# A first norm whose squares are added in pairs on GpSimd, and an inverse root in nine instructions

## The chip, the core and the metric

The kernel runs on one core of a Trainium2 chip. The metric is device time in microseconds, the median of several runs of the whole program. Before the change it is 1212.53 us (three runs, 1211.41 to 1212.78).

A core has five engines that run side by side: TensorE (PE; its weight loads are listed as PEld), VectorE (DVE), ScalarE (ACT), GpSimd (POOL) and SyncE (SP), which here issues DMAs. Each works through its own queue in order. A tile that is written by one engine and read by another carries a semaphore between them.

## The reference

Two residual layers on a sequence of 512 tokens with 1024 channels. Layer 0 mixes tokens with a grouped state-space layer (S5), layer 1 with forgetting attention; each is followed by a gated feed-forward layer with a short convolution. Every sub-layer is preceded by an RMS norm that is modulated by a conditioning vector `c`, and the trunk ends with one more norm:

```python
def rmsnorm(x, g):
    x32 = x.astype(jnp.float32)
    y = x32 * lax.rsqrt(jnp.mean(x32 * x32, axis=-1, keepdims=True) + EPS)
    return (y * g.astype(jnp.float32)).astype(x.dtype)

def modulate(x, g, shift, scale):
    return rmsnorm(x, g) * (1.0 + scale) + shift

def adaln_params(c, w, b):
    mod = jax.nn.silu(c) @ w + b
    shift, scale, gate = jnp.split(mod, 3, axis=-1)
    return shift[:, None, :], scale[:, None, :], gate[:, None, :]
...
    h = x
    for i in range(DEPTH):
        shift, scale, gate = adaln_params(c, ada_w[i, 0], ada_b[i, 0])
        hn = modulate(h, norm_g[i, 0], shift, scale)
        m = s5_mixer(hn, ...) if i % 2 == 0 else fox_mixer(hn, ...)
        h = h + gate * m
        ...
        h = h + gate * conv_ffn(hn, ...)
    return rmsnorm(h, final_g)
```

There are five norms: two in each layer and the last one. Each needs, for every token, the sum of the squares of 1024 channels and one over the root of its mean.

## The kernel before

The activations lie in SBUF as `h`, eight tiles of 128 channels by 512 tokens, so that the channels of a token are spread over partitions. A sum over channels is therefore a matmul with ones.

**The first norm.** It stands at the start of the S5 layer (`s5`, from L1080), before anything else can run. SyncE loads `h` in four DMAs of two tiles (L134), a pack of small constants (`rest`), and then the adaptive-norm weights, eight tiles of 512 KB for the scale and eight for the shift (`ada_pe`, the DMAs at L186 in `raw`). ScalarE squares one tile of `h` after another (L1113) into the pool tile `nm_t`, which has two buffers, and TensorE adds the tile into `ps` (`mmp`) with a matmul against a tile of ones (L1114). Every fp32 matmul shows as two MATMUL instructions in the trace, called passes below. ScalarE copies the sum to SBUF (L1116), and four transposes (L1119) bring it to one row per token: `stats`.

VectorE meanwhile works out the parameters of the state-space layer in `s5_params` (L824): an exponential, a sine and a cosine on tiles of 128x32, dozens of short instructions with L701 to L756, which are helper lines. It then interleaves two lists of instructions: the inverse root of the norm (`inv_root`, L386, which reads `stats`) and the turn factors (`s5_turns`, L896). After that come more parameters (L853 to L881, `next(params)`), the scale that is applied to the norm (`ga`, L167, in `ada_columns`), and the eight normed tiles `a_x` (L1130).

TensorE's order behind the transposes is: the scale matmuls (L205, with weights in `raw`), the norm broadcast over partitions (`rms_rows`, L410), the columns of the scale (L157, L162), the first shift matmuls, and then the input projection (L1144), which reads `a_x` two tiles at a time with shift matmuls in between. The weights' tiles `raw`, `w_hi` and `w_lo` are rings of three, five and five buffers, so a shift load can wait for a scale matmul.

The block from L1106 is written under `manual_schedule` for TensorE, ScalarE, VectorE and SyncE: their instructions keep the program's order. GpSimd isn't in that list; at the start it has only memsets, and the first time that it works on tiles otherwise is in the attention layer (L1453, an addition, and L1496).

The pool `tp` (`s5t`) holds temporary tiles of this stage; it is closed before the loop over the S5 groups, and `s5r` takes its room. `s5r` tiles wait for the tiles that lay there.

**The other norms.** They are fed from the residual additions: squares are added on VectorE as they arise (`square`), and `rms_stats` sums with a matmul, for each half of the tokens by itself, at the end of the product before it (`product`, `tail`). The first half's root is broadcast in the middle of the second half's matmuls (L331), the second half's is put off until 12 matmul groups of the next product are out (`finish_norm`). The last norm's second half has nothing behind it: its root scales the output (`norm_out`). `inv_root` is called nine times: once in the first norm on 128x4 values and eight times on 128x2.

`inv_root` begins with an integer estimate of one over the root, improves it with a step of third order and then with a Newton step. Its instructions depend on one another.

Of the kernel before, what the change touches and what calls it, by code (L numbers as in the profile page):

```python
# [8 lines left out]
F32 = mybir.dt.float32  # L9
# [3 lines left out]
ALU = mybir.AluOpType  # L13
# [4 lines left out]
P = 128  # L18
D = 1024
KT = D // P  # L20
S = 512
# [52 lines left out]
class Trunk:  # L74
# [311 lines left out]
    def inv_root(self, ps, nb, log=None):  # L386
        v, r, t, y = (self.small.tile([P, nb], I32 if n == "r" else F32, name=f"rs_{n}") for n in "vrty")
        e = self.nc.vector
        f = r.bitcast(F32)
        steps = (  # L390
            lambda: e.tensor_scalar(v, ps, 1.0 / D, EPS, op0=ALU.mult, op1=ALU.add),
            lambda: e.tensor_scalar(r, v.bitcast(I32), -0.5, float(0x5F3759DF), op0=ALU.mult, op1=ALU.add),
            lambda: e.tensor_tensor(t, f, f, ALU.mult),
            lambda: e.tensor_tensor(t, t, v, ALU.mult),
            lambda: e.scalar_tensor_tensor(t, t, -1.25 / 0.375, t, op0=ALU.add, op1=ALU.mult),
            lambda: e.tensor_scalar(t, t, 0.375, 1.875, op0=ALU.mult, op1=ALU.add),
            lambda: e.tensor_tensor(y, f, t, ALU.mult),
            lambda: e.tensor_tensor(t, y, y, ALU.mult),
            lambda: e.tensor_tensor(t, t, v, ALU.mult),
            lambda: e.tensor_scalar(t, t, -0.5, 1.5, op0=ALU.mult, op1=ALU.add),  # L400
            lambda: e.tensor_tensor(y, y, t, ALU.mult),
        )
        in_turn(steps) if log is None else log.extend(steps)
        return y
# [268 lines left out]
def in_turn(*logs):  # L673

    order = sorted(((n + 0.5) / len(l), i, n) for i, l in enumerate(logs) for n in range(len(l)))
    for _, i, n in order:
        logs[i][n]()
# [104 lines left out]
class S5(Trunk):  # L782
# [297 lines left out]
    def s5(self, i, nxt):  # L1080
        nc, tc = self.nc, self.tc
# [4 lines left out]
        with ExitStack() as stack:  # L1086
# [4 lines left out]
            ones = keep.tile([P, P], F32, name="s5_ones")  # L1091
            nc.vector.memset(ones, 1.0)
            self.s5q = spool("s5q", stack)
            with ExitStack() as start:
                tp = spool("s5t", start)
                w = {}

                def load_w(m):
                    w[m] = self.raw([P, KT, P], self.io["s5_w_in"][m], m % 3)

                self.rot = keep.tile([P, 2, G // 2, B], F32, name="s5_rot")
                nc.gpsimd.memset(self.rot[:, 0, :, 0:1], 1.0)
                nc.gpsimd.memset(self.rot[:, 1, :, 0:1], 0.0)
                zero = tp.tile([L - 1, CG * GM], F32, name="s5_zero")
                nc.gpsimd.memset(zero, 0.0)
                with tc.manual_schedule(engines={ENG.PE, ENG.Activation, ENG.DVE, ENG.SP}):  # L1106
                    self.load_x(self.act)
                    self.load_rest()
                    self.s5_planes(keep)
                    ps = self.mm.tile([P, S], F32, name="mmp")  # L1110
                    for k in range(KT):
                        sq = self.tmp.tile([P, S], F32, name="nm_t")
                        nc.scalar.activation(sq, self.h[:, k, :], AF.Square)  # L1113
                        nc.tensor.matmul(ps, ones, sq, start=(k == 0), stop=(k == KT - 1))  # L1114
                    rows = self.tmp.tile([P, S], F32, name="nm_t")
                    nc.scalar.activation(rows, ps, AF.Copy)  # L1116
                    stats = self.aux.tile([P, NB, P], F32, name="aux")
                    for b in range(NB):
                        nc.tensor.transpose(stats[:, b], rows[:, b * P:(b + 1) * P], self.ident)  # L1119
                    params = self.s5_params(keep, tp, self.first["s5_prm"], stats[:, :, 0])  # L1120
                    y = next(params)
                    scale = self.ada_pe(i, (1,), late=True)
                    for _ in range(KT // 2):
                        next(scale)
                    rb = self.rms_rows(y, NB)
                    next(params)
                    next(scale)
                    x = self.act.tile([P, KT, S], F32, name="a_x", tag="a_hi")
                    for k in range(KT):
                        nc.vector.scalar_tensor_tensor(  # L1130
                            x[:, k], self.h[:, k], self.ga[i][:, k:k + 1], rb, op0=ALU.mult, op1=ALU.mult
                        )

                    shift = self.ada_pe(i, (0,), late=True)
                    ps = self.mm.tile([P, S], F32, name="mmp")
                    for k in range(KT):
                        if k % 2 == 0:
                            next(shift)
                        if k == 0:
                            load_w(0)  # L1140
                        if k == 6:
                            self.s5_consts(keep, tp)
                            self.s5_signs_b()
                        nc.tensor.matmul(ps, w[0][:, k, :], x[:, k], start=(k == 0), stop=(k == KT - 1))  # L1144
                    next(shift)
                    load_w(1)
                    nc.sync.dma_start(self.rr[:, 0::2], self.io["s5_c"])
                    nc.sync.dma_start(
                        self.z[:, P:, :].rearrange("m j r -> j m r"), zero[:, None, :].to_broadcast([L - 1, KT, CG * GM])
                    )  # L1150
                    for k in range(2):
                        nc.scalar.activation(x[:, k], x[:, k], AF.Identity, bias=self.par[i][:, k:k + 1])
                    col = self.aux.tile([P, 1], F32, name="aux")
                    for k in range(KT):
                        last_mm = nc.tensor.matmul(
                            col, w[0][:, k, :], self.par[i][:, k:k + 1], start=(k == 0), stop=(k == KT - 1)
                        )
                    shifted = self.small.tile([P, 1], F32, name="u_shift")
                    nc.scalar.activation(shifted, col, AF.Copy)
                    first = self.tmp.tile([P, L, B], F32, name="uf", tag="nm_t")  # L1160
                    nc.scalar.activation(first, ps.rearrange("p (b j) -> p j b", j=L), AF.Identity, bias=shifted)
                    for k in range(2, KT):
                        nc.scalar.activation(x[:, k], x[:, k], AF.Identity, bias=self.par[i][:, k:k + 1])
                    behind = [self.s5_signs_c(), next(params), self.s5_tables(slice(0, G // 2), 0, 3), last_mm.ins]
# [42 lines left out]
            ps = self.aux.tile([KT, P], F32, name="aux")  # L1207
# [63 lines left out]
        with tc.tile_pool(name="s5b", bufs=1, reuse_waits="tile") as pool:  # L1271
# [15 lines left out]
            after, y = nxt  # L1287
# [358 lines left out]
```

## Time and profile before

| | |
|---|---|
| median of three runs | 1212.53 us (1211.41 to 1212.78) |
| profiled execution, its own time | 1215.46 us |
| its span, first to last instruction | 1213.7 us |
| TensorE busy | 1183.8 us (98%), 7793 instructions |
| VectorE busy | 1004.6 us (83%), 1872 instructions |
| ScalarE busy | 610.0 us (50%) |
| GpSimd busy | 85.8 us (7%) |
| first matmul of the first norm | 6.57 us |
| inverse root of the first norm begins | 17.57 us |
| first normed tile begins (L1130) | 26.23 us |

The table's last three rows are starts in the profiled execution, counted from its first instruction. The time of an execution is a little longer than its span, since work lies around it. Busy shares are means over stages with different limits, so the first 45 us have to be read by themselves, engine by engine: which instruction waits, and for whom. In a row of a timeline the first number is the start, the second the length; in brackets stand the idle time just before it on its engine and what ended it.

### The profile page before, as it was taken

The numbers are of one execution on the slowest core, as the hardware profiler recorded it, in microseconds if no ns is written. First come the engines' busy times: TensorE is split into PE (matmuls) and PEld (weight loads), VectorE is DVE, ScalarE is ACT, GpSimd is POOL, SyncE is SP. The second block draws the span as 40 slices with busy tenths as digits, with TensorE's granted clock in tenths as the row PEclk, the third lists the DMA queues.
The fourth block names the chain that finished last, engine by engine and source line by source line (L and its number), as shares of the span: only waits on it lengthen the run. The fifth ranks groups of instructions, "written<-read, shape, count | busy, mean of one in ns | idle before, by whom it ended". The sixth has DMA issues, their size and how long they took to land.

```text
span 1213.7 us, 20336 instructions
## 1 busy us (share of the span) xinstructions
PE 1183.8 (98%) x7793; PEld 1015.9 (84%) x7793; DVE 1004.6 (83%) x1872; ACT 610.0 (50%) x1156; POOL 85.8 (7%) x145
## 2 busy tenths in 40 slices
PE   6999999999999999999999999999999999999997
PEld 2566678898988899789899888878989999999987
DVE  7799987689899988899788578876899887888865
ACT  3554565335545453445443565764466554555543
POOL 0000000100000000000000343520000000000000
PEclk9899999999999999999999999999999999999999
DMA  9588787531364544544435453432213332333331
GB/s 356 188 266 258 245 271 253 202 99 53 122 204 156 179 163 155 161 159 130 131 125 194 162 173 134 150 109 88 89 55 111 117 121 84 104 103 109 109 100 70
DMA packets 74513, 183.81 MB, mean 151 GB/s; under 512 B 23232, under 2 KB 25632, under 8 KB 73392
## 3 DMA queue, kind: packets, MB, share of 16 engines
q1 hardware_dynamic: 68367, 161.02, 40.5%
q0 software_dynamic: 5760, 20.97, 5.4%
q8 instruction: 61, 1.00, 0.3%
q10 hardware_dynamic: 288, 0.52, 0.1%
q14 instruction: 37, 0.30, 0.1%
HBM read 175.57 MB, written 6.92 MB: 150 GB/s over the span
## 4 chain that ended last, share of the span: by engine, by line
PE 62%; issue 26%; DVE 4%; DMA 4%; POOL 2%; ACT 1%; SPq 0%; POOLq 0%; DVEq 0%; ACTq 0%
PE mmp L294 25%; PE mmp L550 11%; PE aux L550 4%; PE mmp L1174 3%; PE mmp L1366 3%; PE mmp L1203 2%; PE aux L1505 1%; PE aux L1525 1%; POOL ada_raw L233 1%; PE aux L1065 1%; PE mmp L205 1%; DMA ada_raw<-in_ada_t 1%; PE aux L978 1%; PE aux L1057 1%; DVE w_lo L278 1%
## 5 line engine op out<-in xcount | busy, mean ns | idle before, releaser
L278 DVE TENSOR_TENSOR w_lo<-raw,w_hi 128x1024 fp32r<-128x1024 f32 (+4 forms) x173 | 183.2, 1064 | 37.6 <-ACT w_hi L277 37.1
L277 ACT ACTIVATE w_hi<-raw 128x1024 fp32r<-128x1024 f32 (+4 forms) x173 | 154.8, 905 | 102.0 <-PE mmp L294 44.5
L294 PE MATMUL mmp<-ghi,w_hi 128*128 128x512 f32 (+1 forms) x392 | 145.1, 370 | 0.0
L294 PE MATMUL mmp<-ghi,w_lo 128*128 128x512 f32 (+1 forms) x392 | 144.3, 368 | 0.7 <-DVE w_lo L278 0.5
L294 PE MATMUL mmp<-glo,w_hi 128*128 128x512 f32 (+1 forms) x392 | 144.6, 369 | 0.0
L294 PE MATMUL mmp<-a_hi,w_hi 128*128 128x512 f32 (+1 forms) x376 | 138.4, 371 | 1.5 <-ACT a_hi L433 1.5
L294 PE MATMUL mmp<-a_hi,w_lo 128*128 128x512 f32 (+1 forms) x376 | 136.1, 362 | 0.3 <-DVE w_lo L278 0.3
L294 PE MATMUL mmp<-a_lo,w_hi 128*128 128x512 f32 (+1 forms) x376 | 135.7, 362 | 0.0
L550 PE MATMUL mmp<-w_hi 128*128 128x256 f32 x396 | 109.9, 278 | 3.0 <-ACT nm_h L557 2.5
L550 PE MATMUL mmp<-w_hi,w_lo 128*128 128x256 f32 x396 | 109.7, 278 | 0.7 <-DVE w_lo L278 0.7
L550 PE MATMUL mmp<-w_lo,w_hi 128*128 128x256 f32 x396 | 109.5, 277 | 0.0
L557 ACT ACTIVATE nm_h<-mmp 128x256 f32<-128x256 f32 x99 | 37.2, 381 | 108.3 <-PE mmp L550 108.3
L278 DVE TENSOR_TENSOR w_lo<-sums,w_hi 128x1024 fp32r<-128x1024 f32 x74 | 90.1, 1220 | 0.0
L277 ACT ACTIVATE w_hi<-sums 128x1024 fp32r<-128x1024 f32 x74 | 77.0, 1054 | 25.3 <-DVE sums L518 23.4
L294 PEld LDWEIGHTS mmp<-ghi,w_lo 128*128 128x128 f32 x392 | 74.2, 189 | 13.9 <-DVE w_lo L278 1.4
L294 PEld LDWEIGHTS mmp<-ghi,w_hi 128*128 128x128 f32 x392 | 74.2, 189 | 11.9 <-ACT w_hi L277 0.6
L294 PEld LDWEIGHTS mmp<-glo,w_hi 128*128 128x128 f32 x392 | 74.2, 189 | 11.0
L294 PEld LDWEIGHTS mmp<-a_hi,w_hi 128*128 128x128 f32 x376 | 70.2, 188 | 13.2 <-ACT a_hi L433 1.9
L294 PEld LDWEIGHTS mmp<-a_hi,w_lo 128*128 128x128 f32 x376 | 70.6, 188 | 12.5 <-DVE w_lo L278 1.3
L294 PEld LDWEIGHTS mmp<-a_lo,w_hi 128*128 128x128 f32 x376 | 70.7, 188 | 9.7
L362 DVE SCALAR_TENSOR_TENSOR h<-mmp,par,h 128x512 f32<-128x512 f32 (+1 forms) x100 | 68.1, 683 | 11.8 <-PE mmp L294 11.6
L550 PEld LDWEIGHTS mmp<-w_hi 128*128 128x128 f32 x396 | 74.5, 188 | 3.6 <-ACT nm_h L557 2.9
(319 smaller groups left out, 3082.2 us busy)
## 6 DMA issues: line engine op xcount, KB each, us to landing
raw<-in_w_up SPq DMA_DIRECT2D x88, 512.0 KB, 3.4
raw<-in_ada_w SPq DMA_DIRECT2D x40, 512.0 KB, 6.4
ada_raw<-in_ada_t POOLq DMA_DIRECT2D x40, 512.0 KB, 3.9
nf<-nfd SPq DMA_DIRECT2D x8, 1152.0 KB, 7.8
raw<-in_fox_qk SPq DMA_DIRECT2D x16, 512.0 KB, 3.6
raw<-in_w_down SPq DMA_DIRECT2D x24, 320.0 KB, 3.2
rawd<-in_w_down SPq DMA_DIRECT2D x24, 256.0 KB, 3.3
raw<-in_w_down SPq DMA_DIRECT2D x16, 384.0 KB, 3.4
```

Of the source, the lines that this page charges most:

```text
L205: self.last_mm = nc.tensor.matmul(ps[32 * qq:32 * qq + 32, :], self.sc32[:, k, :], w[:, q * S:(q + 1) * S], start=(step is steps[0]), stop ...
L233: (nc.gpsimd if late else nc.sync).dma_start(ws[n], src)
L277: nc.scalar.activation(hi, src, AF.Copy)
L278: return nc.vector.tensor_tensor(lo, src, hi.bitcast(F32), ALU.subtract)
L294: self.last_mm = self.nc.tensor.matmul(o, wt, xt[:, cols], start=(k == 0 and n == 0), stop=(k == nk - 1 and n == 2),)
L362: add = self.nc.vector.scalar_tensor_tensor(self.h[:, m, cols], ps, self.par[i][:, 16 + m:17 + m], self.h[:, m, cols], op0=ALU.mult, op1=A ...
L550: self.last_mm = nc.tensor.matmul(o, wt[:, k], xt[:, k], start=(first and k == 0 and n == 0), stop=(k == H - 1 and n == 2), skip_group_che ...
L557: a = nc.scalar.activation(t, o, AF.Copy)
L978: nc.tensor.matmul(ps[:, :, cols], x[:, q, r].rearrange("p c j -> p (c j)"), both[:, :, planes, q, :], start=(r == 0), stop=(r == 1), skip ...
L1174: nc.tensor.matmul(ps, w[m][:, k, :], x[:, k], start=(k == 0), stop=(k == KT - 1))
L1203: nc.tensor.matmul(gps[m], wt, xt[:, k], start=(k == 0 and part == 0 and xt is yhi), stop=(k == KT - 1 and part == 1))
L1366: self.last_mm = nc.tensor.matmul(ps[q, b][:, :n], xt[:, k, tb], wt, start=(k == 0 and i == 0), stop=(k == KT - 1 and i == 2),)
```

## The change

In the first norm every second square is added to the one before it by GpSimd, in place, and only the sums go to TensorE: four matmuls instead of eight. The squares move from `nm_t` (two buffers, in the pool `tmp`) to a tile of their own, `s5_sq`, with four buffers in `tp`.

In `inv_root` two multiplications by constants are left out and two pairs of instructions become one: the polynomial of the first step is kept without its factor `a` = 0.375, and the Newton step makes up for it, with 1.5 a and 0.5 a^3 in place of 1.5 and 0.5. What is computed is the same but for rounding. This applies to all nine calls.

```diff
@@ inv_root
+        a = 0.375
         steps = (
             lambda: e.tensor_scalar(v, ps, 1.0 / D, EPS, op0=ALU.mult, op1=ALU.add),
             lambda: e.tensor_scalar(r, v.bitcast(I32), -0.5, float(0x5F3759DF), op0=ALU.mult, op1=ALU.add),
             lambda: e.tensor_tensor(t, f, f, ALU.mult),
             lambda: e.tensor_tensor(t, t, v, ALU.mult),
-            lambda: e.scalar_tensor_tensor(t, t, -1.25 / 0.375, t, op0=ALU.add, op1=ALU.mult),
-            lambda: e.tensor_scalar(t, t, 0.375, 1.875, op0=ALU.mult, op1=ALU.add),
-            lambda: e.tensor_tensor(y, f, t, ALU.mult),
+            lambda: e.scalar_tensor_tensor(t, t, -1.25 / a, t, op0=ALU.add, op1=ALU.mult),
+            lambda: e.scalar_tensor_tensor(y, t, 1.875 / a, f, op0=ALU.add, op1=ALU.mult),
             lambda: e.tensor_tensor(t, y, y, ALU.mult),
-            lambda: e.tensor_tensor(t, t, v, ALU.mult),
-            lambda: e.tensor_scalar(t, t, -0.5, 1.5, op0=ALU.mult, op1=ALU.add),
-            lambda: e.tensor_tensor(y, y, t, ALU.mult),
+            lambda: e.scalar_tensor_tensor(t, t, -0.5 * a ** 3, v, op0=ALU.mult, op1=ALU.mult),
+            lambda: e.scalar_tensor_tensor(y, t, 1.5 * a, y, op0=ALU.add, op1=ALU.mult),
         )
@@ s5
                     ps = self.mm.tile([P, S], F32, name="mmp")
                     for k in range(KT):
-                        sq = self.tmp.tile([P, S], F32, name="nm_t")
+                        sq = tp.tile([P, S], F32, name="s5_sq", bufs=4)
                         nc.scalar.activation(sq, self.h[:, k, :], AF.Square)
-                        nc.tensor.matmul(ps, ones, sq, start=(k == 0), stop=(k == KT - 1))
+                        if k % 2:
+                            nc.gpsimd.tensor_tensor(sq, sq, even, ALU.add)
+                            nc.tensor.matmul(ps, ones, sq, start=(k == 1), stop=(k == KT - 1))
+                        even = sq
```

## The prediction

> **What bounds the kernel now.** I first read the windows view for the whole run, cut where the first norm's consequences end, then TensorE's waits, then the timelines of the first 62 us, engine by engine.
>
> ```profile
> 43.00:196.00 153.00, 152.31 (x1112) 103.09 (x1112) 130.87 (x198) 85.58 (x237) 1.28 (x2) 0.98 0.80 254
> 196.00:1214.00 1018.00, 998.21 (x6540) 898.74 (x6539) 837.94 (x1499) 511.47 (x897) 81.86 (x121) 0.99 0.40 130
> ```
>
> The columns are window, length, then busy time of PE, PEld, DVE, ACT and POOL, the clock, DMA share and GB/s. From 43 us on TensorE is busy 152.31 of 153 us and then 998.21 of 1018: whatever moves the start of that work moves the end by as much. Now the stretch before, where the change is:
>
> ```profile
> 6.57 9.62 PE L1114 MATMUL mmp<-nm_t,s_ones 128*128 128x512 f32 x16 [6.57 <-ACT nm_t L1113]
> 27.03 2.71 PE L1144 MATMUL mmp<-a_x,raw 128*128 128x512 f32 x4 [2.19 <-DVE a_x L1130]
> ...
> 5.89 1.15 ACT L1113 ACTIVATE nm_t<-h 128x512 f32<-128x512 f32 x2 [1.37 <-DMA h<-in_x]
> 14.38 0.63 ACT L1113 ACTIVATE nm_t<-h 128x512 f32<-128x512 f32 x1 [0.23 <-PE mmp L1114]
> ...
> 14.66 0.19 DVE L907 SCALAR_TENSOR_TENSOR s_turn<-s_si 128x32 f32<-128x32 f32 x1
> 17.57 0.16 DVE L391 TENSOR_SCALAR rs_v<-aux 128x4 f32<-128x4 f32 x1 [2.71 <-PE aux L1119]
> ...
> 26.04 0.16 DVE L167 SCALAR_TENSOR_TENSOR ga<-aux,rest 128x8 f32<-128x8 f32 x1
> 26.23 5.35 DVE L1130 SCALAR_TENSOR_TENSOR a_x<-h,ga,aux 128x512 f32<-128x512 f32 x8
> ```
>
> A row gives start, length, engine, line. The first two squares are ready at 7.04 (5.89 + 1.15); later ones, up to 14.38, wait for TensorE to leave one of their two buffers. TensorE sums the eight tiles from 6.57 to 16.19 (two passes a tile, x16). ScalarE's copy and four transposes follow, and 1.38 us later VectorE can begin the inverse root (17.57). VectorE had been done with its own work at 14.85 and sat idle 2.71 us; that is the only place where the norm is waited for. From 17.57 it has no gap: 8.47 us of inverse root, turn factors and parameters, up to `ga` at 26.04; then the normed tiles, and TensorE, idle for 2.19 us, starts L1144 at 27.03. So the path is: norm sum, 1.38, VectorE 8.47, TensorE to the end.
>
> **The change part by part.** (1) TensorE sums 4 tiles instead of 8, so 8 of 16 passes go. (2) Four GpSimd additions of 128x512 come in front of them, each between a square and its matmul. (3) The squares get four buffers instead of two. (4) Eleven VectorE instructions become nine, at each of nine inverse roots.
>
> *The price of a pass and of an addition.*
>
> ```profile
> 7.59 0.33 PEld L1114 LDWEIGHTS mmp<-nm_t,s_ones 128*128 128x128 f32 x1 [0.52 <-ACT nm_t L1113]
> 8.44 0.33 PEld L1114 LDWEIGHTS mmp<-nm_t,s_ones 128*128 128x128 f32 x1 [0.52 <-issue]
> ...
> 11.06 0.19 PEld L1114 LDWEIGHTS mmp<-nm_t,s_ones 128*128 128x128 f32 x1 [0.59 <-ACT nm_t L1113]
> 11.48 0.19 PEld L1114 LDWEIGHTS mmp<-nm_t,s_ones 128*128 128x128 f32 x1 [0.23 <-issue]
> ...
> L1453 POOL TENSOR_TENSOR nf<-nf,rest x16: 1285/1444/2355, 679.4 to 805.0; 128x512 f32<-128x512 f32 x16
> L1453 POOLq MODIFY_POOL_CONFIG  x2: 7/7/7, 660.2 to 660.2; - x2
> ...
> 3.27 0.10 POOL L822 MEMSET s_mask<- 128x1 f32 x1
> 659.91 0.31 POOL L1417 MEMSET phi<- 128x256 f32 x1 [9.96 <-DVE lf_out L727]
> 679.41 2.54 POOL L1453 TENSOR_TENSOR nf<-nf,rest 128x512 f32<-128x512 f32 x2 [19.18 <-DMA nf<-nfd]
> ```
>
> Passes stand 0.85 us apart at first and 0.43 from about 10.5 us on, 3.9 us after TensorE began. A GpSimd addition of just this shape takes 1.285 at least, 1.44 in the median; the first two took 2.54 together. I take 1.3.
>
> The two MODIFY_POOL_CONFIG rows matter more. They stand in the GpSimd queue where its first addition comes, straight behind the last memset (659.91 + 0.31 = 660.22); memsets and DMA issues went before without them. In the changed kernel the first addition is in the first norm, so I expect the pair there, behind the last opening memset, at 3.37. Their own rows say 7 ns, but not when GpSimd can add afterwards: before the change 19.2 us of waiting for `nf` (660.22 to 679.41) covered it. So the price lies between 0 and 19.2 us. The nearest rows are fetches begun in the same opening stretch:
>
> ```profile
> rest<-in_rest SPq DMA_DIRECT2D x1, 204.0 KB, 7.1
> ...
> raw<-in_ada_w SPq DMA_DIRECT2D x6, 512.0 KB, 9.1
> ...
> 10.00:20.00 10.00, 9.31 (x41) 3.11 (x41) 7.05 (x65) 3.74 (x6) 0.00 (x0) 1.00 0.98 388
> ```
>
> The load issued at 3.18 us lands after 7.1, those issued from 5 to 10 us after 9.1, with the DMA engines 98% busy. I take 9.1, as the pair is two steps, and keep 0 and 19.2. The Trainium skill, "GPSIMD Engine Reference", section Instruction dispatch, gives 5.95 us for such a load of code behind MODIFY_POOL_CONFIG; no row here can show it. By it the first addition would start at 9.3 us, which is the second rival's case.
>
> *The norm.* First addition at 3.37 + 9.1 = 12.5, with squares 1 to 4 long ready. Additions 12.5 to 13.8 and 13.8 to 15.1; the first pair of passes 13.85 to 15.55, the second to 17.25 (0.85 a pass, TensorE having just started). Square 6 overwrites the tile that the first pair reads: with 0.3 us for completion and 0.63 for the square it is there at 16.5; third addition to 17.85. Square 8 waits for the second pair likewise: 18.2; fourth addition to 19.55. By then passes are 0.43 (13.85 + 3.9 = 17.75), so the last pair runs 19.6 to 20.45, and with 0.25 for its end the sum stands at 20.7 instead of 16.19: **+4.5 us**. Behind the waiting squares on ScalarE's queue stands only the copy of this sum. Behind the fourth pair on TensorE are the transposes and the scale matmuls of L205, and behind those, on SP's queue, the shift loads that want their buffers. These are needed late enough: the last one is issued at 25.0 and lands 8.6 later, and its matmuls come at 36.36; both ends move together.
>
> ```profile
> raw<-in_ada_w SPq DMA_DIRECT2D x1, 512.0 KB, 8.6
> ...
> 36.36 1.06 PE L205 MATMUL mmp<-raw,s_sc 128*32 128x512 f32 x8
> ```
>
> *VectorE beside the additions.*
>
> ```profile
> 731.88 3.55 POOL L1453 TENSOR_TENSOR nf<-nf,rest 128x512 f32<-128x512 f32 x2 [5.36 <-DMA nf<-nfd]
> ...
> 713.78 1.22 DVE L278 TENSOR_TENSOR w_lo<-raw,w_hi 128x1024 fp32r<-128x1024 f32 x1
> 731.96 2.32 DVE L278 TENSOR_TENSOR w_lo<-raw,w_hi 128x1024 fp32r<-128x1024 f32 x1
> 734.20 0.68 DVE L278 TENSOR_TENSOR lo<-mmp,hi 128x512 fp32r<-128x512 f32 x1
> ```
>
> At 731.96 a VectorE instruction with two SBUF inputs takes 2.32 instead of 1.22: it stands still until the addition begun at 731.88 ends, then runs. The second addition in turn waits for it (3.55 for two instead of 2.54). With one input in PSUM it is undisturbed (0.68). The small instructions of 6 to 15 us nearly all read SBUF only, so each addition that meets them may cost VectorE up to 1.25 us, four 5.0: it would then be done at 14.85 + 5.0 = 19.85 instead of 14.85. In the forecast the statistics come at 20.7 + 1.38 = 22.1, later than that; the stall costs nothing. The Trainium skill, "SBUF — State Buffer", section Who interferes with whom, counts one-input instructions in their two-port mode among those that an addition blocks for its whole length. By it the small ones would pay the 5.0 in full; the trace agrees for two inputs (731.96) and has no row for one.
>
> *The nine instructions.*
>
> ```profile
> 1206.27 0.18 DVE rs_t L396
> ...
> 1206.47 0.17 DVE rs_y L397
> ...
> PE aux L410 <- DVE rs_y L401: 0.5, 2, 0.3
> ```
>
> Instructions that need each other stand 0.20 apart. Two fewer give 0.40 after the last matmul, where nothing covers them. For the root of a tail's first half TensorE waits in two places, 0.5 us together; that goes too. The other inverse roots lie behind matmuls and give nothing. In the first norm turn factors fill the gaps between steps, so two instructions are worth about 0.2.
>
> *Buffers.* The two additional tiles lie in a pool that ends before the state-space loop; the first load into its successor is issued at 46.50, long after. Nothing.
>
> ```profile
> 46.50 0.38 SPq L1181 DMA_DIRECT2D u<-s_ud  x1
> ```
>
> *Sum.* Statistics +4.5, first root -0.2, TensorE's two waits -0.5, last root -0.4: **+3.4 us**. The profiled execution took 1215.46 (span 1213.7), 2.9 above the median of the runs, so I put the sum on the median: 1212.5 + 3.4 = **1215.9 us**. With L for the time behind the pair, it is L + 13.0 (3.4 + 8.2 + 1.4) against 17.57, less 1.1: each microsecond of L counts in full above 6.9, and 0.2%, about what a measurement of this kernel can tell from no change (2.4 us), is passed at L = 8.1.
>
> **The rivals.**
>
> *VectorE decides (L under about 7.5).* With 7.1 from the `rest` row the statistics come at 20.1, sum +1.4; with less the blocked VectorE (19.85) sets the end: 19.85 - 17.57 - 1.1 = +1.2, down to L = 0. About 1213.8. For it speaks that the load nearest in time landed soonest; against it the two steps and the full DMA engines.
>
> *The additions are free (the other side).* GpSimd can add at once and the small VectorE instructions slip between. First addition at 7.1, as the second square is ready at 7.04; then four additions with the same buffer waits end the sum at 15.3, statistics at 16.7: -0.9 - 1.1 = -2.0, 1210.5. It decides only if L is under 3.7 and the stall is under 1.8 us of the 5.0. For it speaks only that no instruction of 128x32 beside an addition is in the trace; 731.96 speaks against it.
>
> *A long load.* The cover was 19.2 us, and nothing shows how much of it was used. At L = 12.2 the sum is +6.5, at 19.2 it is +13.5 (1226).
>
> **How the numbers follow.** Forecast (L 7.5 to 11) 0.47, VectorE decides 0.28, long load 0.15, free additions 0.10. Slower by over 0.2%: the long load and most of the forecast, 0.58. Within: VectorE's case, the forecast's lower edge and most of the free additions, 0.36. Faster: 0.06, the free additions with an earlier full clock. The range leaves out the free additions and the long load's upper half: 1213.0 to 1219.0.
>
> **What would show it.** Right: POOL's queue has the MODIFY_POOL_CONFIG pair near 3.4 us, the first addition begins near 12.5 though its square was ready at 7, L391 near 22, L1130 near 30.5, and TensorE's idle time before its first matmul is near 13 us. VectorE's case: additions from 8 to 10 us, small VectorE instructions of over 1 us beside them, L391 near 20 without an idle gap. Free additions: L391 near 16.7. Wrong altogether: the pair not in front of the first norm's additions, or a start that moves by what the end does not.

## The result and the profile after

| | before | after |
|---|---|---|
| median, range, runs | 1212.33 us (1210.24 to 1213.67, 7) | 1216.94 us (1214.83 to 1219.71, 7) |
| profiled execution, its own time | 1215.46 us | 1219.0 us |
| its span | 1213.7 us | 1217.2 us |

The ratio is 1.0034 (1.0018 to 1.005): 4.1 us slower, 2.2 to 6.1. The forecast of 1215.9 and its range hold. The path by which it got there does not, as the rows show. First, from the page of the kernel after, the busy time of each engine, its share of the span and its instructions:

```profile
PE 1182.2 (97%) x7785; PEld 1015.8 (83%) x7785; DVE 1007.7 (83%) x1854; ACT 608.9 (50%) x1156; POOL 92.9 (8%) x149
```

TensorE is busy 1.6 us less than before (1183.8) and the span is 3.5 us longer, so it stands idle 5.1 us more. Its busy time holds a loss too: eight passes fewer, but more of the rest at half clock, as is seen below. Next the additions by their line (nanoseconds, least/median/most, then first and last start) and in GpSimd's timeline:

```profile
L1114 POOL TENSOR_TENSOR s_sq<-s_sq x4: 1262/1266/1269, 6.6 to 12.4; 128x512 f32<-128x512 f32 x4
L1114 POOLq MODIFY_POOL_CONFIG  x2: 11/11/11, 3.3 to 3.3; - x2
```

```profile
6.62 2.54 POOL L1114 TENSOR_TENSOR s_sq<-s_sq 128x512 f32<-128x512 f32 x2 [3.25 <-ACT s_sq L1112]
9.90 1.26 POOL L1114 TENSOR_TENSOR s_sq<-s_sq 128x512 f32<-128x512 f32 x1 [0.74 <-ACT s_sq L1112]
12.42 1.26 POOL L1114 TENSOR_TENSOR s_sq<-s_sq 128x512 f32<-128x512 f32 x1 [1.26 <-ACT s_sq L1112]
```

The pair stands where the prediction put it, at 3.3 us, but GpSimd adds 3.25 us later, at 6.62, and what ends the wait is the square. Nothing like 9.1 us passes. VectorE beside the additions:

```profile
6.53 1.40 DVE L755 TENSOR_SCALAR s_ring<-s_ring 128x32 int32<-128x32 f32 x2
8.05 1.16 DVE L700 TENSOR_TENSOR s_dt<-s_ring 128x32 f32<-128x32 f32 x1
9.98 1.23 DVE L726 SCALAR_TENSOR_TENSOR s_ring<-s_ring,s_th 128x32 f32<-128x32 f32 x1
...
18.82 0.19 DVE L906 SCALAR_TENSOR_TENSOR s_turn<-s_si 128x32 f32<-128x32 f32 x1
18.93 0.15 DVE L392 TENSOR_SCALAR rs_v<-aux 128x4 f32<-128x4 f32 x1
...
27.35 0.16 DVE L167 SCALAR_TENSOR_TENSOR ga<-aux,rest 128x8 f32<-128x8 f32 x1
27.55 0.75 DVE L1132 SCALAR_TENSOR_TENSOR a_x<-h,ga,aux 128x512 f32<-128x512 f32 x1
```

Instructions of 128x32, which take 0.17 to 0.19 us in undisturbed rows (18.82 is one), last 1.16 and 1.23 us beside an addition. VectorE reaches its first turn factor at 18.82 instead of 14.66, 4.16 us later for four additions. The inverse root then begins without idle time, at 18.93 instead of 17.57: of the 4.16 us, the earlier wait for the norm swallows the rest. `ga` and the normed tiles are 1.3 us later. TensorE, after and then before:

```profile
7.94 5.49 PE L1115 MATMUL mmp<-s_sq,s_ones 128*128 128x512 f32 x6 [7.94 <-DVE s_ring L755]
13.74 1.12 PE L1115 MATMUL mmp<-s_sq,s_ones 128*128 128x512 f32 x2 [0.31 <-POOL s_sq L1114]
28.35 3.78 PE L1146 MATMUL mmp<-a_x,raw 128*128 128x512 f32 x4 [3.06 <-DVE a_x L1132]
32.06 1.94 PE L205 MATMUL mmp<-raw,s_sc 128*32 128x512 f32 x8
43.00 2.55 PE L1157 MATMUL aux<-par,raw 128*128 128x1 f32 x16 [0.27 <-ACT par L170]
```

```profile
29.67 1.93 PE L205 MATMUL mmp<-raw,s_sc 128*32 128x512 f32 x8
40.61 2.51 PE L1155 MATMUL aux<-par,raw 128*128 128x1 f32 x16 [0.27 <-ACT par L170]
```

The norm sum ends at 14.86 (13.74 + 1.12), 1.3 us *earlier* than the 16.19 before: the change does to it what it says, and it is no longer waited for. The first projection starts 1.32 us later (28.35 against 27.03), but the L205 group behind it 2.39 later (32.06 against 29.67). The other 1.1 us is the clock, as the windows show (window, length, busy TensorE, granted clock, DMA share, GB/s), after and then before:

```profile
28.00:30.00 2.00, 1.65 (x2) 0.50 1.02 412
30.00:32.00 2.00, 2.00 (x3) 0.50 1.02 416
32.00:34.00 2.00, 2.00 (x10) 0.52 1.06 421
```

```profile
28.00:30.00 2.00, 2.00 (x7) 0.54 1.02 420
30.00:32.00 2.00, 2.00 (x9) 0.61 1.04 420
32.00:34.00 2.00, 2.00 (x12) 1.00 1.00 405
```

Worked out from these shares and the 0.77 that the kernel after was granted from 26 to 28 us, TensorE runs at half clock from 27.1 to 33.9 us after the change, and from 28.2 to 31.6 before. The column product, hence the whole opening, is 2.39 us later. Last, the final root, before and after, from its first step to the scaling of the output:

```profile
1205.28 0.16 DVE L391 TENSOR_SCALAR rs_v<-aux 128x2 f32<-128x2 f32 x1 [0.58 <-PE aux L380]
1207.53 1.41 DVE L469 TENSOR_SCALAR o_tok<-aux,rs_y 128x512 f32<-128x512 f32 x2
```

```profile
1209.24 0.16 DVE L392 TENSOR_SCALAR rs_v<-aux 128x2 f32<-128x2 f32 x1 [1.24 <-PE aux L380]
1211.08 1.41 DVE L468 TENSOR_SCALAR o_tok<-aux,rs_y 128x512 f32<-128x512 f32 x2
```

2.25 us have become 1.84. The last root starts 3.96 us later, not 2.4: the stages between added 1.5 us of waits in this execution (TensorE idle for 12.55 us from 46.0 to 1205.0 before, for 14.04 from 48.4 to 1209.0 after).

### The profile page after: what moved, and what is told of

Same layout as the page of the kernel before. It is cut to its first block, busy times and chain, and to the rows that moved or that the text cites. A ratio compares the mean times of both kernels' runs of the same rounds, so it can differ in the third digit from the quotient of the medians.

```text
span 1217.2 us, 20303 instructions
## 1 busy us (share of the span) xinstructions
PE 1182.2 (97%) x7785; PEld 1015.8 (83%) x7785; DVE 1007.7 (83%) x1854; ACT 608.9 (50%) x1156; POOL 92.9 (8%) x149
## 4 chain that ended last, share of the span: by engine, by line
PE 62%; issue 14%; DVE 14%; DMA 6%; ACT 2%; POOL 1%; DVEq 0%; POOLq 0%; ACTq 0%; SPq 0%
PE mmp L294 26%; PE mmp L549 10%; PE mmp L1176 4%; DVE w_lo L278 4%; PE aux L549 4%; PE mmp L1368 3%; DMA rawd<-in_w_down 2%; PE mmp L1205 2%; DMA raw<-in_w_up 2%; PE aux L1507 1%; PE aux L977 1%; PE aux L1527 1%; DVE conv L601 1%; PE mmp L205 1%; DVE ada_raw L247 1%
## 5 line engine op out<-in xcount | busy, mean ns | idle before, releaser
L277 ACT ACTIVATE w_hi<-sums 128x1024 fp32r<-128x1024 f32 x74 | 77.0, 1055 | 30.4 <-DVE sums L517 25.6
```

The lines of the kernel that those rows point to most:

```text
L277: nc.scalar.activation(hi, src, AF.Copy)
```

## The experiments

Two theories stood at the start. **Blocked**: GpSimd's additions hold VectorE up, and nothing else about them costs. **Load**: the additions are late because of the MODIFY_POOL_CONFIG pair. Two more came up on the way. **Clock**: a longer idle time ahead of the first projection costs TensorE another stretch at half clock. **Absorbed** against **carry**: what the opening loses or gains reaches the end, or is taken back by waits later. Ratios are to the kernel before, run on the same chip.

**Each half of the change alone.** `e1_nine_only` is the kernel before with the nine-instruction root; `e10_nine_again` repeats it. `e2_pairs_only` has the additions and the four buffers with the root of eleven.

```diff
 e1, e10 (cut: the Newton step is changed as shown further up):
-            lambda: e.tensor_scalar(t, t, 0.375, 1.875, op0=ALU.mult, op1=ALU.add),
-            lambda: e.tensor_tensor(y, f, t, ALU.mult),
+            lambda: e.scalar_tensor_tensor(y, t, 1.875 / a, f, op0=ALU.add, op1=ALU.mult),
 e2 (cut: the four buffers and the matmul on the sums come with it):
+                        if k % 2:
+                            nc.gpsimd.tensor_tensor(sq, sq, even, ALU.add)
```

> The nine-instruction inverse root alone, the first norm as before. Both theories on the first norm (GpSimd not able to add for 9 us: 'load'; GpSimd's additions holding VectorE: 'blocked'): nothing of the opening moves but the 0.2 us of the first root, the last root is 0.4 us shorter, TensorE's wait before L410 goes: 0.4 to 1.1 us faster than before. Rival 'tails' (the part of the 3.5 us between the two profiled executions that is not in the opening, about 1 us, comes from the shorter roots moving work in the tails): 1 to 2 us slower than before.

> The additions on GpSimd alone, eleven instructions in the inverse root. 'Blocked': the opening is as in the changed kernel (L391 near 18.9, first normed tile near 27.7, TensorE 2.4 us late at 45 us), the end 0.4 longer, so 3 to 5.5 us slower than before, 0.4 to 1.1 slower than the changed kernel. 'Tails': only 2.5 us slower than before, faster than the changed kernel. 'Load' as forecast would need the first addition at 12.5; the changed kernel's trace has it at 6.6, and it should be there again.

> The nine-instruction root alone, once more, to stand with its first timing (ratio 0.9984, 0.9967 to 1.0). By the rows of the last root (nine steps in 1.77 us against 2.18) and the wait of TensorE that is gone (0.26 and 0.27 us at two places): 0.4 to 1.8 us faster than before, ratio 0.9985 to 0.9997. If the first timing was chance: 1.0 with the interval on both sides.

Measured: nine instructions 0.9984 (0.9967 to 1.0) and 0.9981 (0.9963 to 0.9999), some 2 us faster; additions alone 1.0071 (1.0051 to 1.0091), 8.6 us slower. The loss is all the additions', and the root gives a little back; "tails", which wanted the root slower, is out. The product of the halves, about 1.0053, is just above the upper end of the interval of both together (1.005), but the halves have intervals of their own. `e2` missed: 3 to 5.5 us were expected, and its interval is 6.2 to 11.0. Its opening is as expected, though (column product at 42.77 us, against 43.00 in the kernel after), so the excess arose behind it and is not explained. Both timings of the root came out above what was expected (0.4 to 1.1, then 0.4 to 1.8 us), with intervals that hold most of it.

**The additions without the norm.** `e3_idle_adds` keeps the norm as it was and adds four GpSimd additions on a tile that nobody reads; `e9_eight_idle` has eight of them. They only add work.

```diff
+                    idle = tp.tile([P, S], F32, name="s5_idle")
+                    nc.gpsimd.memset(idle, 1.0)
+                    for _ in range(4):          # 8 in e9
+                        nc.gpsimd.tensor_tensor(idle, idle, idle, ALU.add)
                     ps = self.mm.tile([P, S], F32, name="mmp")
```

> The kernel before, with four GpSimd additions of 128x512 beside it on a tile that nobody reads: the norm's sum, its buffers and its root stay as they are. 'Blocked': VectorE stands still for most of each addition, so its first turn factor comes at 18 to 19.7 instead of 14.7 though the statistics are there at 17.6, the first normed tile at 27.5 to 28.2 instead of 26.2, and the whole is 1.3 to 4 us slower. 'Load': the pair in front of the first addition keeps GpSimd from adding for about 9 us, the first addition comes at 13 or later, and the VectorE work of 6 to 13 us is undisturbed. Since nothing else is waited for, the gap between GpSimd's last memset and its first addition is the time behind the pair: under 'blocked' under 3.3 us.

> The kernel before with eight unread GpSimd additions of 128x512 in the opening instead of the four of the run with four (whose first turn factor on VectorE began at 18.15 us against 14.66 before, its first projection matmul at 27.70). Theory 'blocked' (each addition holds VectorE up by 0.9 to 1.05 us): the first turn factor begins at 21.3 to 22.5 us, a_x at 30 to 31, the first projection matmul near 31, so some 4 us behind the kernel before, and TensorE at half clock behind its idle time. If a delay of the opening reaches the end in full ('carry'): 4 to 6 us slower than before, ratio 1.0033 to 1.005. If the feed-forward stages take part of it back ('absorbed'): 1 to 3 us slower. Rival 'no block' (the four additions' stall was of another origin): the first turn factor near 18.

The timelines of four additions, then of eight:

```profile
3.69 0.16 POOL L856 MEMSET s_pi<- 128x32 f32 x1
3.85 2.19 POOL L1113 TENSOR_TENSOR s_idle<-s_idle 128x512 f32<-128x512 f32 x2
...
18.15 0.19 DVE L907 SCALAR_TENSOR_TENSOR s_turn<-s_si 128x32 f32<-128x32 f32 x1
18.26 0.15 DVE L391 TENSOR_SCALAR rs_v<-aux 128x4 f32<-128x4 f32 x1
```

```profile
21.34 0.19 DVE L907 SCALAR_TENSOR_TENSOR s_turn<-s_si 128x32 f32<-128x32 f32 x1
21.45 0.15 DVE L391 TENSOR_SCALAR rs_v<-aux 128x4 f32<-128x4 f32 x1
...
30.91 2.93 PE L1148 MATMUL mmp<-a_x,raw 128*128 128x512 f32 x3 [1.16 <-DVE a_x L1134]
```

The first addition begins at 3.85, the very end of the last memset (3.69 + 0.16). That settles "load": the price behind the pair is nothing that a row can show. It also shows the block by itself: the first turn factor comes 3.49 us later for four additions and 6.68 for eight (14.66, 18.15, 21.34), 0.87 and 0.84 each, with the norm untouched. The whole is 1.002 (1.0001 to 1.0039) and 1.0064 (1.0038 to 1.0089): 2.4 us and 7.8 us slower. The first projection of the double dose starts at 30.91, 3.9 later than before, as "blocked" wanted; its time is above the expected 4 to 6 us, with an interval (4.6 to 10.8) that holds most of them. So this delay of the opening carries to the end; "absorbed", 1 to 3 us, is out for it.

**The clock.** `e8_after_again` is the kernel after once more. `e5_after_warm` fills the idle time before its first projection with three matmuls whose result is not read.

```diff
+                            junk = self.aux.tile([P, S], F32, name="junk", tag="aux")
+                            for n in range(3):
+                                nc.tensor.matmul(junk, ones, self.h[:, 0, :], start=(n == 0), stop=(n == 2))
```

> The changed kernel once more, beside the next three on the same chip. 'Clock' (VectorE's 1.3 us leave TensorE idle for 3.1 instead of 2.2 us ahead of its first projection matmul, and the granted clock halves for one or two of its steps of 3.4 us more often than before): 3 to 6 us slower than before, half clock between 28 and 33 us, first projection passes 0.85 apart. 'Only VectorE': the difference in the opening stays at 1.3 us at the first projection matmul and the rest of the gap to before is chance that this run needn't repeat: 0.5 to 2 us slower than before.

> The changed kernel with three matmuls (six passes, about 2.6 us) that nobody reads in TensorE's idle time ahead of the first projection matmul. 'Clock': full clock from 24 to 34 us, the first four projection passes take 2.0 instead of 3.8 us, TensorE at its column product 1.1 us (one step) to 1.8 us earlier than in the changed kernel, the whole 1.5 to 3 us faster than it. 'Only VectorE': as the changed kernel or slower, since work is only added.

The kernel after repeats: 1.0026 (1.0008 to 1.0044), 3.2 us slower, with its column product at 43.01. That is in the range of "clock" (3 to 6 us); the interval, 1.0 to 5.3, holds most of "only VectorE" (0.5 to 2) as well, so the rows have to decide. With the fill, TensorE's timeline and then the window:

```profile
25.30 2.84 PE L1145 MATMUL junk<-h,s_ones 128*128 128x512 f32 x6
28.43 1.98 PE L1149 MATMUL mmp<-a_x,raw 128*128 128x512 f32 x4 [0.29 <-DVE a_x L1132]
...
40.42 1.95 PE L1160 MATMUL aux<-par,raw 128*128 128x1 f32 x16 [0.27 <-ACT par L170]
```

```profile
28.00:32.00 4.00, 3.71 (x15) 1.00 1.03 412
```

The projection starts no earlier (28.43), but its four passes take 1.98 instead of 3.78 and the column product comes 2.59 us earlier. The time is 1214.81 against 1217.8 in the same runs, ratio 1.001 (0.9992 to 1.0027) against the 1.0026 above. The intervals overlap, so the times alone don't show the gain; the rows do. TensorE's idle time at the opening costs more than its length.

**The same fill elsewhere.** `e6_before_warm` has two such matmuls in the kernel before, `e11_nine_warm` in the nine-instruction one.

> The kernel before with two such matmuls (four passes, about 1.7 us) in its idle time of 2.2 us. 'Clock': full clock from 24 to 34 us; since the idle time is shorter here, the half clock comes in some executions only, so 0.5 to 1.5 us faster than before, and the lead over the warmed changed kernel is about 1 us (VectorE's 1.3 us less the 0.4 of the last root), not 4. 'Only VectorE': no change or slower.

> The nine-instruction root alone, with two unread matmuls in TensorE's idle time before the first projection. Theory 'clock' (an idle stretch there costs one step of about 3.4 us at half clock, where it falls that way): full clock from 24 to 34 us, 0.5 to 1.5 us faster than the nine-instruction root alone in the same runs. Theory 'absorbed': no difference between the two, within 1 us.

`e6`: 1.0004 (0.9983 to 1.0025), a miss, and its median is 1.0 us above that of `e5` instead of 1 us below. `e11`: 0.9994 (0.9969 to 1.0019); its median is 0.5 us under that of `e10`, its ratio above the 0.9981, which decides nothing. The profile of `e10` says why, in TensorE's timeline and the window:

```profile
27.19 1.98 PE L1143 MATMUL mmp<-a_x,raw 128*128 128x512 f32 x4 [2.19 <-DVE a_x L1129]
...
39.18 1.95 PE L1154 MATMUL aux<-par,raw 128*128 128x1 f32 x16 [0.27 <-ACT par L170]
```

```profile
28.00:32.00 4.00, 4.00 (x15) 1.00 1.04 422
```

In that execution TensorE had idled for 2.19 us before the projection, just as long as in the profile before, and the clock stayed full; with nearly the same start (27.19 against 27.03) its column product came 1.43 us earlier (39.18 against 40.61). So an idle time of this length is followed by a half-clock stretch in some executions and by none in others. In all five profiled executions with additions and without the fill (after, `e2`, `e3`, `e8`, `e9`) the granted clock was 0.50 throughout from 28 to 32 us; of the others without a fill there, only the profile before fell to half clock in those 4 us, for part of them.

**Without the additions.** `e4_four_buffers` is the kernel after with the GpSimd additions taken out: eight squares in four buffers, sixteen passes. `e12_four_again` repeats it. `e7_four_early` also starts TensorE at 1 us with twelve small matmuls whose result is not read.

```diff
                         sq = tp.tile([P, S], F32, name="s5_sq", bufs=4)
                         nc.scalar.activation(sq, self.h[:, k, :], AF.Square)
                         nc.tensor.matmul(ps, ones, sq, start=(k == 0), stop=(k == KT - 1))
 e7, ahead of the loop:
+                    junk = self.aux.tile([P, P], F32, name="junk", tag="aux")
+                    for n in range(12):
+                        nc.tensor.matmul(junk, ones, ones, start=(n == 0), stop=(n == 11))
```

> The changed kernel without the additions: eight squares in four buffers, eight matmuls, nine instructions. 'Blocked': with no GpSimd work VectorE is free at 14.85 again; TensorE need not wait for squares and ends the sum near 13.7 instead of 16.2 (9 passes at 0.85 and 7 at 0.43 from 6.6 on), so L391 comes near 15.1 instead of 17.6, the first normed tile near 24, and the whole is 2.5 to 3.5 us faster than before. Rival: the scale weights, whose last tile TensorE gets at 20.4 in both traces, hold the scale, and the first normed tile comes no earlier than 25: then 1 to 1.5 us faster.

> Eight squares in four buffers, no additions, nine instructions, and twelve small matmuls of the ones tile with itself from 1 us on that nobody reads, so that TensorE's clock is full when the first square comes. 'Clock': passes 0.43 apart from the first square or shortly after it, the sum ends near 11 instead of 14.8 (without them) and 16.2 (before), VectorE goes on without a gap at 14.7 to 14.9, and the first normed tile comes at 23.5 to 24 instead of 26.2: 3 to 5 us faster than before. If the passes are 0.85 apart as before, the early matmuls don't count and it is as the run without them, about 1 us faster than before.

> Four buffers for the squares, no GpSimd additions, nine-instruction root, once more (first timing 0.9985, 0.997 to 1.0001, with an opening 4 to 5 us shorter in its trace). Theory 'carry': 2.5 to 3.5 us faster than before, ratio 0.997 to 0.998. Theory 'absorbed' (what the opening gains is lost in waits of the feed-forward stages): 0 to 1.5 us faster, as in its first timing.

Measured: 0.9985 (0.997 to 1.0001), 0.9997 (0.9977 to 1.0017) and 0.9978 (0.9962 to 0.9995). The first, 1.8 us faster, lies between its two theories, and its interval holds most of both; the second misses; the third, 2.7 us, lies in the range of "carry", with an interval (0.6 to 4.6) that holds most of "absorbed" too. `e4` had its column product at 37.57, 3.0 us before that of the profile before. Why that is worth no more than the root alone, the two traces of this one kernel tell in part. The norm sum of `e4` and of `e12`, each followed by the window of its passes from 9 to 11 us:

```profile
6.14 8.61 PE L1113 MATMUL mmp<-s_sq,s_ones 128*128 128x512 f32 x16 [6.14 <-ACT s_sq L1112]
```

```profile
9.00:11.00 2.00, 2.00 (x6) 1.00 1.04 421
```

```profile
6.61 9.91 PE L1113 MATMUL mmp<-s_sq,s_ones 128*128 128x512 f32 x16 [6.61 <-DVE s_ring L700]
```

```profile
9.00:11.00 2.00, 2.00 (x3) 1.00 1.04 422
```

The windows start alike and end at different counts: six passes in two microseconds against three. In `e4` the passes go from 0.85 us apart to 0.43 at about 9 us, in `e12` at about 12, and its sum ends at 16.52 instead of 14.75 (0.47 us of that is its later start). The clock column says 1.00 in both, so only the spacing of the passes shows it. The code up to there is the same; the moment differs from execution to execution. The Trainium skill, "TensorE: Matmul & The Clock Gate", Part 1, says that the activity window behind the clock runs freely, so that one kernel's number of slow matmuls depends on where the window happens to stand at its start. The traces agree: over the nine executions that begin the sum between 5.7 and 6.6 us, with no matmul ahead of it, the change comes between 8.6 and 12.2 us. The profile before had it at about 11; `e6`, the same code up to the projection, had it at 8.6, and its root began here:

```profile
16.03 0.16 DVE L391 TENSOR_SCALAR rs_v<-aux 128x4 f32<-128x4 f32 x1 [1.16 <-PE aux L1119]
```

That is 1.54 us before the 17.57 of the profile before; 0.9 us of it is an earlier start of the sum (5.67 against 6.57), the rest the earlier change of rate.

A second place matters more. Behind the column product come 16 passes of the next projection (L1173), then the first matmuls of the state-space loop (L977). Here are both in `e4`, with its windows from 40 to 44 us, then in `e10`:

```profile
39.48 8.73 PE L1173 MATMUL mmp<-a_x,raw 128*128 128x512 f32 x16
48.05 2.34 PE L977 MATMUL aux<-s_both,x 128*128 128x160 f32 x16
...
40.00:42.00 2.00, 2.00 (x4) 0.50 0.32 125
42.00:44.00 2.00, 2.00 (x4) 0.68 0.88 272
```

```profile
41.10 7.11 PE L1173 MATMUL mmp<-a_x,raw 128*128 128x512 f32 x16
48.05 2.34 PE L977 MATMUL aux<-s_both,x 128*128 128x160 f32 x16
```

`e4` is 1.6 us ahead of `e10` at the column product (37.57 against 39.18) and level with it at 48.05, since it ran at half clock for 3.4 us in between and `e10` not at all. `e7`, with its column product at 37.54, met such a stretch too and reached L977 at 48.02; so did `e11`, there at 49.05. `e12` and `e1` had none and were there at 48.20 and 48.07. In the profile before TensorE was at half clock for 6.8 us there (41.8 to 48.6), besides the 3.4 us further up, and came to this row (its L978) at 52.75, 4.7 us behind `e10`, which differs from it by the root alone and whose first projection had started 0.16 us later. So most of what these openings seemed to gain on the profile before is the clock of single executions, and the leads of `e4` and `e7` on the nine-instruction root alone are gone at 48 us. Whether an earlier opening brings the half clock on there, or the two met it by chance, is open. The expectations took two single executions for two kernels; a median over a dozen runs mixes them, and that it therefore shows little of such a lead is inferred, not shown by a run of its own.

Behind this row `e7` loses more than `e10` does: its profiled execution took 1218.31 us against 1212.16. A part of that lies in the stretch from 330 to 410 us, where TensorE waited more (busy 74.86 of 80 us, against 76.67 in `e10`), but these windows vary between kernels that do the same work there:

```profile
330.00:410.00 80.00, 79.21 (x512) 1.00 0.54 175
```

```profile
330.00:410.00 80.00, 76.48 (x501) 1.00 0.54 174
```

```profile
330.00:410.00 80.00, 74.86 (x484) 0.98 0.52 171
```

These are before, after and `e7`. Whether an early start of the opening provokes these waits is open.

## Why the prediction was right in its time and wrong in its path

The forecast was 3.4 us and 4.1 were measured, but that agreement is luck: no row shows the term that made up the forecast, and of what cost the time one part was priced at nothing and another, the clock behind the idle time, was left out.

*The price behind the pair, 9.1 us: wrong, and this is the step that failed.* It was put between 0 and 19.2 and taken near a DMA's landing time. The kernel after shows at most 3.25 us, which the square's lateness explains, and `e3` shows none. The Trainium skill's 5.95 us ("GPSIMD Engine Reference", section Instruction dispatch), cited beside it for a load of code, shows in no run here either; the start at 9.3 us that it gives would have been the case "VectorE decides", the first of the rivals and not the second. With the price falls the norm sum's +4.5 us: the sum ended at 14.86, not 20.7.

*The stall of VectorE, "the stall costs nothing": wrong, as it hung on the late norm.* Its size was forecast well: up to 1.25 us for each addition, 5.0 in all, measured 4.16 in the kernel after. The instructions with one input paid too: those in the row at 6.53 have one each, and the two took 1.40 us instead of 0.30. The rival "VectorE decides" is the case that came about, with L near 0, GpSimd's additions from 6.6 us and the root without an idle gap; it expected the root at 19.85 and it came at 18.93.

*What made the rival's +1.2 us too small.* Its own terms give 1.3 us at the projection (28.35 against 27.03) less 0.9 for the roots. Missing were two. One is the clock: another 1.1 us at half rate behind the longer idle time, shown by the windows and by `e5`. Against the profile before that makes 1.5 us (1.3 + 1.1 - 0.9). The other is the ground that it was counted from: the profile before was an execution with 10.2 us at half clock between 28 and 49 us. The five profiled executions with additions and without the fill (after, `e2`, `e3`, `e8`, `e9`) had 13.6 us or more of it up to 53 us and came to the state-space loop at 54.7 to 57.4 us. Five without either (`e1`, `e4`, `e7`, `e10`, `e12`) had 0 to 3.4 us and came to it at 48.0 to 48.2. Counted from those, the kernel after (55.14) is some 7 us late at this place; counted from the profile before (52.75), 2.4. The measured 2.2 to 6.1 lies between, but how often the kernel before meets the half clock is not known, so the 4.1 us are not accounted for to the last microsecond: the profile also has 1.5 us in waits between the opening and the last root, which vary between executions.

*The start of the sum.* The forecast let the passes reach their full rate 3.9 us after TensorE began. In the profile before they were still 0.85 us apart at 11.0, so it was 4.5 us, and other executions have 3 to 5.7. In the forecast's sum that changes nothing, as its last pair of passes stood at 19.6, 5.75 us behind the first.

*The nine instructions: right on two of three.* The last root fell from 2.25 to 1.84 us, the 0.4 forecast. Both waits of TensorE for a tail's root are gone; the list of waits has one left, in the first norm:

```profile
PE aux L409 <- DVE rs_y L400: 0.7, 1, 0.7
```

The 0.2 us of the first root came out as 0.05: 8.42 us from the root to `ga` (18.93 to 27.35) instead of 8.47. Alone the root is worth some 2 us by its timings, with intervals from 0 to 4.5, so 0.9 is not contradicted.

*The buffers, nothing: borne out.* `e4` and `e12` against `e1` and `e10` differ by them alone, and the ratios are the same within their intervals.

*"Whatever moves the start of that work moves the end by as much": borne out for delays* (`e2`, `e3` and `e9` lost at least what their openings had lost against the profile before), not for the lead of `e7`.

*Free additions and the long load: out.* In the first the stall had to be under 1.8 us; the second needs a price behind the pair.

## What to carry to other kernels

An addition moved to GpSimd is not free because GpSimd is idle: look for what VectorE does in those microseconds, and charge it most of the length of each addition where it works on SBUF alone (here 0.84 to 1.04 us of 1.08 to 1.27). Here the sum of squares did end 1.3 us sooner than in the profile before, though not sooner than in `e6`, which has no additions (14.65 against 14.86), and the chain beside it became 4.2 us longer; its slack had been 2.71 us in the profile before and 1.16 in `e6`. And the opening differed by 4.7 us between two executions (before, `e10`) through the clock and not through the root that sets the two kernels apart, more than the change costs: read the granted clock of both before one trace is set against another. Of this change the half to keep is the inverse root: alone it ran at 0.9984 and 0.9981, the best that these runs found together with the four buffers of `e12` (0.9978).

## What had not been expected of the hardware

- GpSimd's first addition of the program starts at once behind its MODIFY_POOL_CONFIG pair: 3.85 us, the end of the last memset (`e3`).
- A train of 0.19 us instructions of VectorE loses 0.84 to 1.04 us for each 128x512 addition of 1.08 to 1.27 us: 4.16 us for four, 6.68 us for eight back to back. Instructions with one input are held up like those with two.
- The additions on one unread tile took 1.08 us in the median (`e3`: 1038/1080/1097 ns), those of the norm, whose operands are two tiles, 1.27 (1262/1266/1269). Why was not tried.
- The start of a matmul train runs at half rate (0.85 us a pass) for 3 to 5.7 us, by execution, and the clock column reads 1.00 in that time. `e4` and `e12`, one kernel, took 8.61 and 9.91 us for the same sum.
- An idle time of TensorE of 2.2 to 2.4 us was followed by half clock in one execution and not in others (before; `e10`, `e12`); with 2.6 to 3.1 us ahead of the projection (`e3`, after), the half clock lasted past 32 us.
- Half clock came in stretches of 3.4, 6.8 or 10.2 us in the openings: 28.2 to 31.6 and 41.8 to 48.6 before, 27.1 to 33.9 and 44.2 to 51.0 after, 25.6 to 35.8 in `e9`. The later one stands behind the 128x1 matmuls of the column product; why some executions lack it was not tried.
